# A gated DeltaNet layer: the state's update from plain transposed keys and a scaled y

## The chip, the cores and the metric

The kernel runs on one core of one Trainium2 chip. The metric is the device time of one execution in microseconds (us). The engines meant below are TensorE (PE in the rows, PEld where it loads weights), VectorE (DVE), ScalarE (ACT), GpSimd (POOL) and the queue of SyncE (SP), which issues most DMAs. Each engine executes its own instructions in a fixed order and waits on semaphores for the others.

## The reference, cut to what matters

The layer has two branches on the same normalised input: a Fourier branch, and a bidirectional gated DeltaNet with 8 heads of 128 channels. The context (256 tokens) is scanned first; the latent tokens (1024) start from its final states. Cut to one head, one direction and one chunk, the scan is this:

```python
def step(s, xs):
    q_c, k_c, u_c, w_c, qk_c, gc_c = xs
    v_new = u_c - einsum('cd,de->ce', w_c, s)
    o_c = einsum('cd,de->ce', q_c * exp(gc_c)[:, None], s) + einsum('ij,je->ie', qk_c, v_new)
    g_last = gc_c[-1]
    k_dec = k_c * exp(g_last - gc_c)[:, None]
    s = s * exp(g_last) + einsum('cd,ce->de', k_dec, v_new)
    return s, o_c
```

The last product sums over the tokens c of the chunk. The factor exp(g_last - gc_c) belongs to a token, so it may stand on the key's row or on the row of v_new: the sum is the same.

## The kernel before, in words

The kernel takes chunks of 128 tokens: 8 latent chunks (NCH) and 2 context chunks (NXC), 10 units (NU) in all. The big projections are products in three float32r passes (L127, L130 and L133, 128x512 each), which accumulate in two double-bank buffers called main. The work of a head's DeltaNet is float32.

Each head goes through three stages in `deltanet` (L671), which yields wherever TensorE may take other work:

1. **zp.** For five pairs of chunks, K K^T and K Q^T (L688) are multiplied by decay factors E into the tile zp (L692). The factors come by DMA (L708), get a mask on GpSimd (L710) and an exponential on ScalarE (L714).
2. **inverse** (L724). VectorE inverts 32x32 blocks in a loop of 30 steps (L748, L751), and TensorE puts the blocks together.
3. **scan** (L818). Ten steps t. Each serves direction 0 (d=0) from the front and direction 1 from the end, with a state S[d] each. t=0 and 1 are the context's chunks.

One scan step before the change, by line: L840 multiplies the keys by S; L842 (VectorE) makes R of it; L850 multiplies the queries by S, from t=2 on, into one PSUM bank for both directions (qs2); L854 multiplies the inverted block by R; L856 (ScalarE) copies that product, y, from PSUM into zp (at t=0 with a factor -1); L861 (ScalarE, t=2 to 5) or L863 (VectorE, t=6 to 9) scales the product of L850 into the output acc; L869 multiplies the keys kdec by y; L873 (VectorE) makes the new S of it; from t=6 on, L881 adds both directions' inner part out of zp. At t=9 no state is updated.

kdec is the tile of transposed keys times ce, the factor of the token: L699, on GpSimd, one instruction for each direction (128x1280), issued after the five pairs of zp and before the inverse. The plain transposed keys, ktok (L617), come from PSUM by VectorE (L622), and `k_norms` (L644 to 654) makes ce out of the decays, the gates and the keys' norms. These run for head h+1 while head h is worked on. Both ktok and kdec have one buffer.

PSUM has four banks of a ring called s for all the small products; a product gets the bank that was used four allocations before, once its readers are done.

What sets the order: `weave` (L248) hands out the projections of the next head and of the merge gates as fill between the steps of the head's own chain, by a table of times (STEPS, times a head's RATES). That gives the order in the code; the compiler's planner then orders each engine's instructions with its own costs, so that ready work further down in the code may be put ahead. In the trace the masks (L710) for head 1's first four pairs run before 376 us, although the code issues them inside head 0's scan, which begins at 413 us. The weights of the fill are loaded by `weight` (L178): DMA on SP (L182), a cast on ScalarE (L188), a subtraction on GpSimd (L189).

Of the kernel before, what the change touches and what calls it, by code (L numbers as in the profile page):

```python
# [8 lines left out]
F32 = mybir.dt.float32  # L9
# [54 lines left out]
class Net:  # L64
# [18 lines left out]
    def rsqrt(self, pool, x, shape, tag):  # L83
        """1 / sqrt(x) of a small float32 tile: Newton steps from an integer seed."""
        v = self.nc.vector
        y = pool.tile(shape, F32, tag=tag + "y", name=tag + "y")
        t = pool.tile(shape, F32, tag=tag + "t", name=tag + "t")
        v.tensor_scalar(out=t.bitcast(I32), in0=x.bitcast(I32), scalar1=1, scalar2=None,
                        op0=ALU.arith_shift_right)
        v.tensor_scalar(out=y.bitcast(I32), in0=t.bitcast(I32), scalar1=-1, scalar2=1597463007,  # L90
                        op0=ALU.mult, op1=ALU.add)
        for _ in range(3):
            v.tensor_tensor(out=t, in0=y, in1=y, op=ALU.mult)
            v.scalar_tensor_tensor(out=t, in0=t, scalar=-0.5, in1=x, op0=ALU.mult, op1=ALU.mult)
            v.scalar_tensor_tensor(out=y, in0=t, scalar=1.5, in1=y, op0=ALU.add, op1=ALU.mult)
        return y

    def split(self, x, hi, lo, eng=None):
        """x = hi + lo, both of float32r's width."""
        self.nc.scalar.copy(out=hi, in_=x)  # L100
        (eng or self.nc.gpsimd).tensor_tensor(out=lo, in0=x, in1=hi.bitcast(F32), op=ALU.subtract)  # L101

    def split2(self, x, hi, lo, n):
        """The same by halves, on two engines."""
        for c, e in ((slice(0, n // 2), self.nc.gpsimd), (slice(n // 2, n), self.nc.vector)):
            self.split(x[:, c], hi[:, c], lo[:, c], e)

    def operand(self, part):
        """One part of eight blocks of 128 rows by 1024, in the place of the last such."""
        return [self.hpool.tile([P, NT], F32R, tag=f"{part}{k}", name=f"{part}{k}") for k in range(KT)]  # L110

    def turns(self):
        """VectorE and GpSimd by turns."""
        self.turn = not self.turn
        return self.nc.vector if self.turn else self.nc.gpsimd

    def mm3(self, ps, lh, ll, rh, rl, first, last):
        """ps += (lh + ll)^T (rh + rl) in three float32r passes."""
        mm = self.nc.tensor.matmul
        mm(ps, lhsT=lh, rhs=rh, start=first, stop=False)  # L120
        mm(ps, lhsT=lh, rhs=rl, start=False, stop=False)
        mm(ps, lhsT=ll, rhs=rh, start=False, stop=last)

    def mm3y(self, ps, lh, ll, rh, rl, first, last):
        """The same, giving TensorE away in between."""
        mm = self.nc.tensor.matmul
        mm(ps, lhsT=lh, rhs=rh, start=first, stop=False)  # L127
        if FINE == 3:
            yield 0.217
        mm(ps, lhsT=lh, rhs=rl, start=False, stop=False)  # L130
        if FINE == 3:
            yield 0.217
        mm(ps, lhsT=ll, rhs=rh, start=False, stop=last)  # L133
        yield 0.65 if FINE == 1 else 0.216

# [1 line left out]
    def constants(self):  # L137
# [21 lines left out]
        # adds up four blocks of 32 rows  # L159
# [32 lines left out]
    def latent(self, src, rhs, k, done):  # L192
        """A block of weights times the latent tokens' operand: quanta of PE work, then done(PSUM)."""
# [24 lines left out]
    def plain(self, f):  # L218
        """Work that needs no weights, as a job."""
# [5 lines left out]
    def after(self, f):  # L225
        """The same for work in several parts."""
        return None, 0, lambda w: f()

    def stream(self, jobs, first=None):
        """Run jobs in order, the weights of the next one under way; first: the first one's, if they are."""  # L230
# [17 lines left out]
    def weave(self, lead, fill, rate, times):  # L248
        """fill takes TensorE between the lead's steps: after each, rate times its entry of times."""
# [12 lines left out]
    def pe_add(self, x, rows, ec, eng=None):  # L262
        """x += the tokens' position code: the grid's rows in one half of the channels, its columns in the other."""
# [3 lines left out]
    def head(self, first):  # L267
# [6 lines left out]
        with ExitStack() as es:  # L274
# [8 lines left out]
            # rows' codes in three parts of bfloat16's width, and which of them a token takes  # L283
# [31 lines left out]
            def parted(i):  # L315
                """A group's weights in two parts, in the place of operands to come or of tokens gone."""
# [8 lines left out]
            # silu of c and c_ctx  # L325
# [5 lines left out]
            # in two parts, all four columns against either part of the weights  # L331
# [49 lines left out]
            # scale and shift as columns, two contraction blocks at a time  # L381
# [42 lines left out]
            def narrow(ps, h, l, kt):  # L424
                """Rows 0-31 take two of the three products, 32-63 the third."""
# [45 lines left out]
    def tables(self, bd, sp):  # L471
# [5 lines left out]
        # turned, and the two parts added up  # L477
# [18 lines left out]
        # log1p(e) = 2 atanh(e / (2 + e))  # L496
# [15 lines left out]
        # running sums within a chunk, in each direction's order, and the whole chunk's  # L512
# [13 lines left out]
        # sums as rows  # L526
# [12 lines left out]
    def conv(self, pool, ps, blk, dst, n, view=None, bufs=4, parts=1, away=False):  # L539
        """dst = 2 silu(conv(ps)) along the free dim."""  # L540
# [43 lines left out]
    def tok(self, src, units):  # L584
        """Transposes of up to four chunks into one PSUM bank."""
# [10 lines left out]
    def qkv_jobs(self, h, G):  # L596
        """The head's projections and all of its preparation that needs no decay matrix."""
# [18 lines left out]
        def k_tok():  # L616
            G.ktok = dn.tile([P, NU, P], F32, tag="ktok", name="ktok")  # L617
# [11 lines left out]
        def q_tok():  # L629
# [9 lines left out]
            # the guard of the output's norm, in the units of the unnormalised q  # L639
# [4 lines left out]
        def k_norms():  # L644
# [7 lines left out]
            for d in range(2):  # L652
                v.tensor_tensor(out=G.c[:, d], in0=self.b[:, 8 * d + h], in1=r2, op=ALU.mult)
                v.tensor_tensor(out=G.ce[:, d], in0=self.edl[:, 8 * d + h], in1=G.c[:, d], op=ALU.mult)

# [15 lines left out]
    def deltanet(self, h, G, side):  # L671
        """Yields wherever TensorE may take other work meanwhile."""
# [3 lines left out]
        # decay factors, zero outside the triangle; [Z | P] = [K K^T | K Q^T] c E  # L676
# [20 lines left out]
        G.kdec = dn.tile([P, 2, NU, P], F32, tag="kdec", name="kdec")  # L697
        for d in range(2):
            gp.tensor_tensor(out=G.kdec[:, d], in0=G.ktok, in1=G.ce[:, d].unsqueeze(2).to_broadcast([P, NU, P]), op=ALU.mult)  # L699
# [3 lines left out]
    def decays(self, h, p):  # L703
        """A pair of chunks' decay factors, zero outside the triangle, in either direction."""
# [11 lines left out]
    def collect(self, G, lo, hi):  # L716
        """Diagonal 32-blocks of some chunks side by side, direction 1 transposed: all upper triangles."""
# [6 lines left out]
    def inverse(self, G, side):  # L724
        """Z -> V = -(I + strict Z)^-1 in place, both directions of all chunks."""
# [7 lines left out]
        # one block a partition: X[block, column, row]  # L733
# [4 lines left out]
        # a column's entries need only columns as they were: even and odd columns by turns  # L738
# [22 lines left out]
        # the halves' inverses, transposed  # L761
# [6 lines left out]
        # 32 -> 64  # L768
# [19 lines left out]
        # 64 -> 128  # L788
# [29 lines left out]
    def scan(self, h, G):  # L818
# [9 lines left out]
        for t in range(NU):  # L828
            if h + 1 < HEADS and t in EARLIER:
                self.decays(h + 1, EARLIER.index(t))  # L830
            # the context's two chunks, then the latent tokens'; direction 1 from the ends
# [20 lines left out]
            for d, u in enumerate(us):  # L852
                ps = self.s()[:, :P]
                mm(ps, lhsT=zp[:, d, u], rhs=R[d], start=True, stop=True)  # L854
                y[d] = zp[:, d, u]
                act.mul(out=y[d], in_=ps, mul=-1.0) if new else act.copy(out=y[d], in_=ps)  # L856
# [9 lines left out]
            if not last:  # L866
                for d, u in enumerate(us):
                    ps = self.s()[:, :P]
                    mm(ps, lhsT=G.kdec[:, d, u], rhs=y[d], start=True, stop=True)  # L869
# [23 lines left out]
    def finish(self, h, G):  # L893
        """RMS norm over the head's channels, q's norm with it; the gate. Yields between parts."""
# [34 lines left out]
    def fourier_jobs(self, sp, ctx):  # L929
# [19 lines left out]
        def fold(g, ps):  # L949
# [9 lines left out]
            # the cosine and sine sums of even k, then their even and odd ones; those of odd k  # L959
# [109 lines left out]
    def gate_rows(self, sp):  # L1069
        """adaLN's gate, halved, on every partition."""  # L1070
# [19 lines left out]
        # silu doubled: acc is twice the product  # L1090
# [7 lines left out]
    def heads_out(self):  # L1098
        """All heads' outputs as the operand of the next product, and its first blocks: jobs."""
# [18 lines left out]
    def tail(self):  # L1118
# [3 lines left out]
        with ExitStack() as es:  # L1122
# [21 lines left out]
            def gated(kt):  # L1144
                """Rows of the output weights, times adaLN's gate."""
# [21 lines left out]
            def source(i):  # L1167
                """Token tile i: what its product is added to, and where that goes, by column pieces."""
# [215 lines left out]
```

## Time and profile before

| what | value |
|---|---|
| three runs | 1408.75, 1407.92, 1408.34 us, median 1408.34 us |
| the profiled execution: its span, which is all that the page gives of its time | 1409.0 us |
| PE busy | 1296.9 us, 92% |
| DVE busy | 967.8 us, 69% |
| ACT busy | 555.9 us, 39% |
| POOL busy | 451.1 us, 32% |
| mean granted TensorE clock | 0.959 |

An engine's share is its busy time over the span and says nothing of what the other engines waited for. The views used below are the page, groups of instructions by line (with least, middle and greatest duration), sums of waits, the busy time in stretches, the timeline and the chain of work that ended last, which is followed back from the last instruction.

### The profile page before, as it was taken

How to read it: one execution, taken by the hardware profiler on the slowest of the kernel's cores; microseconds unless marked ns; L12 is line 12 of the kernel's file. 1: busy time of each engine (PE TensorE's matmuls, PEld its weight loads, DVE VectorE, ACT ScalarE, POOL GpSimd, SP SyncE). 2: the span in 40 equal slices, each digit the busy share in tenths (PEclk: the TensorE clock that was granted, in tenths of full speed). 3: DMA queues.
4: the chain of work that ended last, by engine and by line, in shares of the span. 5: the costliest groups of instructions: out<-in, count | busy, mean ns of one | idle time of the engine just before them, and what ended most of it. 6: DMA issues, size and time to landing. Idle time of an engine off the chain costs nothing.

```text
span 1409.0 us, 22686 instructions
## 1 busy us (share of the span) xinstructions
PE 1296.9 (92%) x8274; PEld 1050.7 (75%) x8274; DVE 967.8 (69%) x2664; ACT 555.9 (39%) x1499; POOL 451.1 (32%) x358
## 2 busy tenths in 40 slices
PE   7899999999789989889899998988998999999997
PEld 1487787887678768768777876876876877888786
DVE  6776554308876965984894795697697494744997
ACT  2643333335444444443544444345354343521200
POOL 3532332135523222430440332223243122234610
PEclk9999999999899999989998999999998999999999
DMA  8434332342211211311311211121120032375431
GB/s 316 152 97 119 115 111 91 125 169 78 65 39 44 69 46 48 88 61 38 83 58 56 53 62 66 50 79 54 35 79 31 31 113 75 120 264 162 160 124 60
DMA packets 51892, 129.91 MB, mean 92 GB/s; under 512 B 6242, under 2 KB 18915, under 8 KB 51780
## 3 DMA queue, kind: packets, MB, share of 16 engines
q1 hardware_dynamic: 44496, 114.02, 26.1%
q10 hardware_dynamic: 7284, 14.45, 3.0%
q8 instruction: 65, 1.06, 0.3%
q14 instruction: 47, 0.39, 0.1%
HBM read 105.29 MB, written 23.15 MB: 91 GB/s over the span
## 4 chain that ended last, share of the span: by engine, by line
PE 50%; DVE 33%; DMA 6%; ACT 5%; POOL 3%; issue 3%; ACTq 0%; SPq 0%; DVEq 0%; POOLq 0%
PE main L127 8%; PE main L133 8%; PE main L130 8%; DVE X L751 7%; DVE B L748 6%; DMA E<-gr 3%; PE s L854 3%; PE s L869 3%; PE s L840 2%; PE s L881 2%; PE s L850 2%; DVE cv L553 2%; POOL E L710 2%; DVE cv L552 2%; PE main L120 2%
## 5 line engine op out<-in xcount | busy, mean ns | idle before, releaser
L127 PE MATMUL main<-h,whi 128*128 128x512 f32 x1008 | 424.8, 421 | 6.2 <-DVE cv L553 6.2
L133 PE MATMUL main<-h,wlo 128*128 128x512 f32 x1008 | 410.8, 408 | 0.1
L130 PE MATMUL main<-l,whi 128*128 128x512 f32 x1008 | 410.2, 407 | 0.0
L127 PEld LDWEIGHTS main<-h,whi 128*128 128x128 f32 x1008 | 196.2, 195 | 42.9 <-ACT th L554 5.8
L189 POOL TENSOR_TENSOR wlo<-wraw,whi 128x1024 fp32r<-128x1024 f32 x48 | 127.7, 2660 | 307.1 <-ACT whi L188 295.0
L133 PEld LDWEIGHTS main<-h,wlo 128*128 128x128 f32 x1008 | 195.5, 194 | 40.5 <-POOL wlo L101 0.5
L130 PEld LDWEIGHTS main<-l,whi 128*128 128x128 f32 x1008 | 196.0, 194 | 32.8
L751 DVE TENSOR_TENSOR X<-X,B 128x110 f32<-128x110 f32 (+27 forms) x472 | 120.6, 292 | 0.0
L748 DVE TENSOR_TENSOR B<-X 128x110 f32<-128x110 f32 (+27 forms) x472 | 111.8, 274 | 0.0
L101 POOL TENSOR_TENSOR wlo<-wraw,whi 128x512 fp32r<-128x512 f32 (+1 forms) x40 | 49.8, 1245 | 180.9 <-ACT whi L100 172.2
L710 POOL TENSOR_TENSOR E<-E,mask 128x256 f32<-128x256 f32 x80 | 67.2, 866 | 89.7 <-DMA E<-gr 62.0
L188 ACT CAST whi<-wraw 128x512 fp32r<-128x512 f32 x96 | 59.4, 623 | 79.7 <-PE main L130 71.4
L100 ACT CAST whi<-wraw 128x512 fp32r<-128x512 f32 (+1 forms) x80 | 44.7, 575 | 109.1 <-PE main L130 73.5
L554 ACT ACTIVATE th<-cv 128x512 f32<-128x512 f32 (+1 forms) x64 | 36.9, 576 | 124.6 <-DVE cv L553 124.4
L714 ACT ACTIVATE E<-E,nG 128x128 f32<-128x128 f32 x160 | 52.7, 392 | 68.2 <-POOL E L710 67.7
L692 DVE SCALAR_TENSOR_TENSOR zp<-s,c,E 128x256 f32<-128x256 f32 (+1 forms) x160 | 64.5, 452 | 21.6 <-ACT E L714 14.6
L101 DVE TENSOR_TENSOR wlo<-wraw,whi 128x512 fp32r<-128x512 f32 (+1 forms) x40 | 36.9, 923 | 61.4 <-ACT whi L100 48.2
L699 POOL TENSOR_TENSOR kdec<-ktok,ce 128x1280 f32<-128x1280 f32 x16 | 37.0, 2326 | 130.6 <-PE s L869 128.3
L873 DVE SCALAR_TENSOR_TENSOR S<-S,egl,s 128x128 f32<-128x128 f32 x128 | 40.0, 344 | 54.9 <-PE s L869 53.2
L856 ACT COPY zp<-s 128x128 f32<-128x128 f32 x144 | 36.3, 273 | 80.3 <-PE s L854 80.3
L552 DVE SCALAR_TENSOR_TENSOR cv<-main,cst,cv 128x511 f32<-128x511 f32 (+1 forms) x48 | 35.3, 735 | 39.6 <-ACT cv L549 39.6
L842 DVE SCALAR_TENSOR_TENSOR R<-s,eG,vt 128x128 f32<-128x128 f32 x144 | 45.3, 347 | 22.5 <-PE s L840 19.1
(343 smaller groups left out, 2560.3 us busy)
## 6 DMA issues: line engine op xcount, KB each, us to landing
wraw<-in_win SPq DMA_DIRECT2D x72, 512.0 KB, 3.5
E<-gr SPq DMA_DIRECT2D x40, 256.0 KB, 4.7
wmod<-in_wm SPq DMA_DIRECT2D x32, 256.0 KB, 5.4
x<-in_x SPq DMA_DIRECT2D x8, 512.0 KB, 5.4
wgate<-in_wg SPq DMA_DIRECT2D x8, 512.0 KB, 3.9
yf<-yf ACTq DMA_DIRECT2D x8, 512.0 KB, 2.8
rfy<-yf SPq DMA_DIRECT2D x8, 512.0 KB, 4.5
af<-rfy SPq DMA_DIRECT2D x8, 512.0 KB, 2.6
```

Source lines behind the costliest of these rows:

```text
L101: (eng or self.nc.gpsimd).tensor_tensor(out=lo, in0=x, in1=hi.bitcast(F32), op=ALU.subtract)
L127: mm(ps, lhsT=lh, rhs=rh, start=first, stop=False)
L130: mm(ps, lhsT=lh, rhs=rl, start=False, stop=False)
L133: mm(ps, lhsT=ll, rhs=rh, start=False, stop=last)
L188: self.nc.scalar.copy(out=hi[:, i:i + n], in_=raw[:, i:i + n])
L189: self.nc.gpsimd.tensor_tensor(out=lo[:, :k], in0=raw[:, :k], in1=hi[:, :k].bitcast(F32), op=ALU.subtract)
L552: v.scalar_tensor_tensor(out=x[:, a:hi], in0=ps[:, a - 1:hi - 1], scalar=w(0), in1=x[:, a:hi], op0=ALU.mult, op1=ALU.add)
L692: v.scalar_tensor_tensor(out=o, in0=ps.rearrange("p (a i) -> p a i", a=W), scalar=G.c[:, d, u:u + 1], in1=e[:, d, i].unsqueeze(1).to_broad ...
L710: nc.gpsimd.tensor_tensor(out=e[:, d], in0=e[:, d], in1=self.mask[:, d].unsqueeze(1).to_broadcast([P, 2, P]), op=ALU.add)
L714: nc.scalar.activation(out=e[:, d, i], in_=e[:, d, i], func=AF.Exp, bias=self.nG[:, 8 * d + h, u:u + 1])
L748: v.tensor_tensor(out=B, in0=X[:, c0::2, l:l + 1].to_broadcast([P, w, l]), in1=X[:, l:l + 1, :l].to_broadcast([P, w, l]), op=ALU.mult)
L751: v.tensor_tensor(out=X[:, c0::2, :l], in0=X[:, c0::2, :l], in1=B, op=ALU.subtract)
```

## The change

The diff also strips comments and docstrings throughout; that part is left out here. ktok gets a second buffer, since it is now read until the end of the scan. ce gets a factor -1 in the two columns that t=0 uses. kdec goes. In the scan, y becomes a tile of its own with four buffers, written by ScalarE from PSUM with the factor ce of each token (each partition), for all steps but the last; the unscaled copy into zp remains for the latent chunks, as a second reading of the same bank. L869's product takes ktok and the scaled y.

```diff
         def k_tok():
-            G.ktok = dn.tile([P, NU, P], F32, tag="ktok", name="ktok")
+            G.ktok = dn.tile([P, NU, P], F32, tag="ktok", name="ktok", bufs=2)
...
                 v.tensor_tensor(out=G.ce[:, d], in0=self.edl[:, 8 * d + h], in1=G.c[:, d], op=ALU.mult)
 
+            for d, u in enumerate((NCH, NU - 1)):
+                v.tensor_scalar(out=G.ce[:, d, u:u + 1], in0=G.ce[:, d, u:u + 1], scalar1=-1.0, scalar2=None, op0=ALU.mult)
+
...
             yield
-        G.kdec = dn.tile([P, 2, NU, P], F32, tag="kdec", name="kdec")
-        for d in range(2):
-            gp.tensor_tensor(out=G.kdec[:, d], in0=G.ktok, in1=G.ce[:, d].unsqueeze(2).to_broadcast([P, NU, P]), op=ALU.mult)
         yield from self.inverse(G, side)
...
                 mm(ps, lhsT=zp[:, d, u], rhs=R[d], start=True, stop=True)
-                y[d] = zp[:, d, u]
-                act.mul(out=y[d], in_=ps, mul=-1.0) if new else act.copy(out=y[d], in_=ps)
+                if not last:
+                    y[d] = dn.tile([P, P], F32, tag="y", name="y", bufs=4)
+                    act.mul(out=y[d], in_=ps, mul=G.ce[:, d, u:u + 1])
+                if t >= NXC:
+                    act.copy(out=zp[:, d, u], in_=ps)
...
                     ps = self.s()[:, :P]
-                    mm(ps, lhsT=G.kdec[:, d, u], rhs=y[d], start=True, stop=True)
+                    mm(ps, lhsT=G.ktok[:, u], rhs=y[d], start=True, stop=True)
```

## Rows read from the trace of the kernel before

**Rows 1.** The page: the chain that ended last, by engine.
```profile
PE 50%; DVE 33%; DMA 6%; ACT 5%; POOL 3%; issue 3%; ACTq 0%; SPq 0%; DVEq 0%; POOLq 0%
```

**Rows 2.** Head 1's inverse and scan: us, PE, PEld, DVE, ACT, POOL busy; clock, DMA.
```profile
460.00:500.00 40.00, 35.84 (x155) 28.85 (x153) 39.97 (x144) 17.20 (x51) 11.54 (x10) 0.91 0.24 72
...
520.00:560.00 40.00, 40.00 (x311) 35.12 (x310) 18.65 (x54) 15.93 (x50) 5.68 (x3) 1.00 0.10 34
```

**Rows 3.** By line: kdec; y's copies; ScalarE's scaled reading of PSUM (ns, min/median/max).
```profile
L699 POOL TENSOR_TENSOR kdec<-ktok,ce x16: 2319/2326/2331, 334.3 to 1125.2; 128x1280 f32<-128x1280 f32 x16
...
L856 ACT COPY zp<-s x144: 256/267/360, 417.0 to 1227.2; 128x128 f32<-128x128 f32 x144
...
L861 ACT ACTIVATE acc<-s,eG x64: 367/380/452, 419.5 to 1209.5; 128x128 f32<-128x128 f32 x64
```

**Rows 4.** Sums of waits: who <- whom, us in total, times, longest.
```profile
PEld s L869 <- ACT zp L856: 7.7, 36, 0.6
```

**Rows 5.** Timeline of head 0, t=3: start, duration, instruction, [idle before <- releaser].
```profile
422.47 0.37 ACT L861 ACTIVATE acc<-s,eG 128x128 f32<-128x128 f32 x1 [1.99 <-PE s L850]
...
422.73 0.26 ACT L856 COPY zp<-s 128x128 f32<-128x128 f32 x1
422.88 0.38 ACT L861 ACTIVATE acc<-s,eG 128x128 f32<-128x128 f32 x1
423.04 0.30 PEld L869 LDWEIGHTS s<-zp,kdec 128*128 128x128 f32 x2 [0.20 <-ACT zp L856]
...
423.14 0.28 ACT L856 COPY zp<-s 128x128 f32<-128x128 f32 x1
...
423.29 0.48 PE L127 MATMUL main<-h,whi 128*128 128x512 f32 x1
...
423.61 0.38 PE L869 MATMUL s<-zp,kdec 128*128 128x128 f32 x2
```

**Rows 6.** Timeline of head 1, t=7.
```profile
550.85 0.49 ACT L856 COPY zp<-s 128x128 f32<-128x128 f32 x2 [4.27 <-PE s L854]
...
551.57 0.60 PE L869 MATMUL s<-zp,kdec 128*128 128x128 f32 x4
```

**Rows 7.** Timeline of GpSimd between heads 1 and 2.
```profile
556.70 2.33 POOL L699 TENSOR_TENSOR kdec<-ktok,ce 128x1280 f32<-128x1280 f32 x1 [20.54 <-PE s L869]
558.99 2.36 POOL L189 TENSOR_TENSOR wlo<-wraw,whi 128x1024 fp32r<-128x1024 f32 x1
...
568.55 2.80 POOL L710 TENSOR_TENSOR E<-E,mask 128x256 f32<-128x256 f32 x4 [4.92 <-DMA E<-gr]
```

**Rows 8.** The chain that ended last, at the same place: start, duration, link.
```profile
562.83 0.89 DVE zp L692 x2
563.74 4.68 DMA E<-gr
```

**Rows 9.** Timeline of GpSimd, VectorE and ScalarE ahead of head 0.
```profile
334.31 4.62 POOL L699 TENSOR_TENSOR kdec<-ktok,ce 128x1280 f32<-128x1280 f32 x2 [2.36 <-DVE ce L654]
338.88 2.83 POOL L189 TENSOR_TENSOR wlo<-wraw,whi 128x1024 fp32r<-128x1024 f32 x1
...
337.94 1.54 DVE L562 SCALAR_TENSOR_TENSOR vT<-th,cv 128x512 f32<-128x512 f32 x1
...
341.22 1.04 DVE L562 SCALAR_TENSOR_TENSOR vT<-th,cv 128x512 f32<-128x512 f32 x1
...
335.48 0.62 ACT L188 CAST whi<-wraw 128x512 fp32r<-128x512 f32 x1
```

**Rows 10.** Timeline of VectorE and GpSimd while head 3's keys are normalised.
```profile
619.40 2.32 DVE L88 TENSOR_SCALAR dnrt<-se 128x10 int32<-128x10 int32 x1
...
624.21 0.25 DVE L654 TENSOR_TENSOR ce<-edl,c 128x10 f32<-128x10 f32 x2
...
627.80 0.68 DVE L562 SCALAR_TENSOR_TENSOR vT<-th,cv 128x512 f32<-128x512 f32 x1
...
619.30 2.39 POOL L189 TENSOR_TENSOR wlo<-wraw,whi 128x1024 fp32r<-128x1024 f32 x1
```

## The prediction

> **What bounds the kernel now.** First the chain by engine [rows 1]: half of the span is TensorE, a third VectorE, 5% ScalarE and 3% GpSimd. The two engines whose work the change alters most are thus hardly on the chain, so I read the stages. The stretches [rows 2] show two limits that take turns in each head. In the inverse VectorE is busy 39.97 of 40.00 us and TensorE 35.84. In the scan TensorE is busy 40.00 of 40.00, VectorE 18.65, ScalarE 15.93, GpSimd 5.68, at a granted clock of 1.00. The scan is therefore bound by TensorE's queue as long as fill stands ready for each wait of the chain L840, L842, L854, L856, L869, L873. Whether it always does is told by the sum of waits [rows 4]: L869's weight load waited for y 36 times, 7.7 us in all, 0.21 each, in 72 steps that update a state. Two steps show both kinds. In head 0, t=3 [rows 5], the first y ends at 422.99 and L869 starts at 423.04, 0.20 late; the second y ends at 423.42, and one product of the fill lies between L869's two halves. In head 1, t=7 [rows 6], both copies are done by 551.34 and L869 starts at 551.57: 0.23 us to spare.
>
> **GpSimd: kdec goes.** It is 16 x 2.326 = 37.2 us of GpSimd [rows 3], but what is it worth on the chain? Between heads 1 and 2 [rows 7] kdec waited until the old scan's last reading of it, and the subtraction of the next weights, wlo, stands between its two halves: that wlo comes at most 2.33 us earlier without it, and SP's next load of raw weights, which waits for wlo's reading, with it. GpSimd's next work is the mask at 568.55, which waits for a DMA; that DMA leaves when VectorE releases its buffer at 563.72 [rows 8]. kdec is not what is late there, nor is GpSimd. I take zero for heads 1 to 7; a gain is bounded by one kdec half in the four heads with this pattern, 9.3 us.
>
> Head 0 is different [rows 9]. Its kdec runs from 334.31 to 338.93, and VectorE's v convolution L562 at 337.94 took 1.54 us, against 0.68 elsewhere [rows 10]; the next one, beside wlo (338.88 to 341.71), took 1.04. Without kdec, wlo starts when its cast ends, at 336.10, and ends about 338.5. The first L562 is then done near 338.5 + 0.55 = 339.05 instead of 339.48 (0.43 gained), the second runs free (0.36 gained). The v convolution is on the chain there, ahead of the first product of zp: -0.8 us, between 0 and -1.2 (both excesses, 0.86 + 0.36, gone).
>
> The Trainium skill ("SBUF — State Buffer", section "SBUF: two separate sides") says that GpSimd and VectorE share a pair of ports under an exclusive lock: a VectorE operation with two SBUF inputs, or in a two-port mode, waits for the whole of a GpSimd one. The trace agrees: L88, an instruction of 128x10 elements, took 2.32 us beside a wlo of 2.39 [rows 10]. The rule speaks for a gain wherever such an operation runs beside kdec. In heads 1 to 7 the timeline has only L873, L842, L863, L882, L568 and L692 there, which read PSUM and keep their usual durations; so the rule adds nothing to the 0.8 us of head 0.
>
> **VectorE: two columns of ce change sign.** Two instructions on one column for each head, 16 in all. The trace has none on one column; the nearest are the two L654 on ten columns, 0.25 us as a pair [rows 10]. I take 0.2 us for the new pair. For heads 1 to 7 they stand in VectorE's queue ahead of the v convolution and the joining of the 64-blocks, on the chain in most of them: 6 x 0.2 = +1.2 us. Bounds: 0 (all in gaps) and 8 x 0.25 = 2.0; one that meets a GpSimd instruction could cost up to 2.3 like L88, and I leave that to the range.
>
> **ScalarE: y scaled, then copied.** Steps t=2 to 8 get two instructions more, 14 for each head, 112 in all: 112 x 0.267 = 30 us more busy time on an engine that is busy 15.93 of 40 us in the scan. The busy time costs nothing by itself; the place in the queue does. Reading PSUM with a factor per partition takes 380 ns against the copy's 267 [rows 3], so the first y comes 0.11 us later. The second y now has the first unscaled copy ahead of it. From the starts in [rows 5], the next instruction begins 0.26 us after a scaled one (422.47 to 422.73) and 0.15 after a copy (422.73 to 422.88). Put into that step: the acc product at 422.47, y at 422.73, the copy at 422.99, the second acc product at 423.14, the second y at 423.40, done at 423.78. Its half of L869 started at 423.61 before and can now start at about 423.83: +0.22. If the planner puts the second acc product behind both copies, the bank of qs2 comes free only when that is done, and the fourth-next allocation is L869's second bank: y at 423.14, copy 423.40, acc 423.55 to 423.93, so 423.98: +0.37. If it puts both y ahead of both copies, only some +0.1 remains.
>
> Where there is 0.23 us to spare, as in [rows 6], this is covered; nothing of L881 moves, since it stands behind L869. Where y is already awaited, in 36 steps, between 36 x 0 and 36 x 0.37 = 13.3 us could show. Another fill product of 0.23 us put into the hole takes most of it, at the price of having less fill later; what stays visible today is 0.21, less than one such product. I take a third of 0.22 + 0.02 = 0.08 for each: +2.9 us. If the cover were gone in all 56 steps from t=2 to 8, it would be 56 x 0.22 = 12.3.
>
> The rest costs nothing: L869 does the same product on other weights, loaded the same way; y has four buffers, two steps' worth; the second ktok is written while the first is read, so the copies L622 wait for nothing new.
>
> **Sum.** Against the span: 1409.0 - 0.8 + 1.2 + 2.9 = 1412.3 us. The median of the runs shown is 0.7 us below that span, so 1411.6 us for the runs.
>
> **The rivals.**
> - *Covered.* The planner moves fill into every hole, as it already does between L869's halves in [rows 5], or puts both y first; what is left is 1.2 - 0.8: 1408.7 us. For it: TensorE has no gap in head 1's scan [rows 2]. Against: y is awaited in half of the steps [rows 4].
> - *Faster, by the ports.* Taking kdec away moves wlo, up to 2.33 us, and where the order of GpSimd's later work shifts against the keys' norms, the 2.1 us that L88 lost (2.32 against the 0.25 of two such small instructions) in heads like that of [rows 10] go: four heads, 8.4 us, so 1411.6 - 8.4 = 1403.2 us; from two heads on it is faster than before. Against: the wlo in question, at 619.30, stands in the inverse behind other GpSimd work, 58 us after kdec. (Were all of kdec's 37.2 us taken off VectorE's share of the chain, it would be 1409.0 - 37.2 - 0.7 = 1371.1 us; only head 0's kdec shows a held-up neighbour, so I give that 0.01, within this rival's chance.)
> - *Slower, by ScalarE's queue.* The copies stand ahead of the second acc product, qs2 is held, and each step from t=2 to 5 is 0.37 us longer with the fill used up: 32 x 0.37 = 11.8, with 9 awaited steps from t=6 on at 0.22 another 2.0: 1409.0 - 0.8 + 1.2 + 13.8 - 0.7 = 1422.5 us. It decides as soon as ten such steps show it (3.7 us). For it: the code has the copies ahead of the acc products. Against: the acc product's bank is ready before y's is [rows 5], and TensorE's fill stands at hand.
> - *The change not doing what it says*: none that I see, since kdec's instructions are simply absent.
>
> **Numbers.** The measurement tells some 0.2% (2.8 us) from no change. Forecast (slightly slower, 1409.5 to 1416): 0.42, of which 0.1 lies within 0.2%. Covered: 0.24, within. Ports: 0.18, faster. ScalarE's queue: 0.16, slower. So faster 0.18, same 0.34, slower 0.48. The range goes from 1404 (just under half of the port rival's gain against today's time) to 1420 (most of ScalarE's queue): about 0.1 is left out at either end.
>
> **What would show it.** In the trace after: no L699; the wait of L869's load for y longer than 7.7 us in all, up to 10 or 11; y at 0.38 us and the second y some 0.25 us later against L854 than before; in head 0, L562 near its 0.68; L88 near 2.3 still. The prediction is wrong if the total of those waits is unchanged or if the stretch from one scan to the next shrinks; if the scan of heads 1 to 4, where fill covers y today, grows by over 1 us each, ScalarE's queue or the planner's order is the cause.

## The result and the profile after

The changed kernel takes 1416.79 us (median of four runs, 1414.57 to 1420.08; the kernel before beside it 1408.13). The ratio is 1.0075, with a 95% interval of 1.0052 to 1.0098: slower by 0.75%. The profiled execution spans 1418.3 us, 9.3 more than before, at a granted clock of 0.961 (0.959 before).

The page of the changed kernel, busy time by engine, then the chain that ended last by engine (against [rows 1]):

```profile
PE 1297.2 (91%) x8274; PEld 1047.4 (74%) x8274; DVE 967.8 (68%) x2680; ACT 586.5 (41%) x1611; POOL 408.8 (29%) x342
...
PE 36%; DVE 23%; DMA 3%; ACT 3%; issue 1%; POOL 1%; DVEq 0%; ACTq 0%; POOLq 0%; SPq 0%
```

GpSimd has lost 42.3 us of busy time (451.1 before) and ScalarE has gained 30.6; TensorE and VectorE do what they did. The chain's shares add up to 67% here, since it was not followed back to the start, so they are not set against [rows 1].

By line of the changed kernel (count, ns min/median/max), against [rows 3]. L857 writes the scaled y, L859 the copy into zp, L864 is what was L861, L657 the change of sign:

```profile
L857 ACT ACTIVATE y<-s,ce x144: 349/368/415, 414.7 to 1231.4; 128x128 f32<-128x128 f32 x144
L857 ACTq EVENT_SEMAPHORE  x104: 17/17/17, 420.4 to 1220.2; - x104
...
L859 ACT COPY zp<-s x128: 255/266/308, 420.7 to 1236.0; 128x128 f32<-128x128 f32 x128
...
L864 ACT ACTIVATE acc<-s,eG x64: 359/398/432, 420.2 to 1216.3; 128x128 f32<-128x128 f32 x64
...
L657 DVE TENSOR_SCALAR ce<-ce x16: 141/154/155, 334.8 to 1078.7; 128x1 f32<-128x1 f32 x16
```

kdec's line is gone. The second row was in nobody's sum: 104 of the 144 scaled readings come with an event of their own in ScalarE's queue. In the program those 104 wait for two things, TensorE's product and an earlier instruction of ScalarE itself, because y's tile is reused in turn; in the kernel before no y has such an event.

The sum of waits of the load of L872 (before: L869) for y, against [rows 4]:

```profile
PEld s L872 <- ACT y L857: 11.1, 44, 1.0
```

That is 3.4 us more. It is only a part. **Where the 9.3 us lie** is told by the stages. Take a head's scan from the first L854 of t=0 to that of t=9:

| scan of head | 0 | 1 | 2 | 3 | 4 | 5 | 6 | 7 | sum |
|---|---|---|---|---|---|---|---|---|---|
| before, us | 27.38 | 34.07 | 34.08 | 34.08 | 34.36 | 30.06 | 26.59 | 35.57 | 256.2 |
| after, us | 29.75 | 34.71 | 34.75 | 34.69 | 34.70 | 31.61 | 28.41 | 36.94 | 265.6 |

The scans have grown by 9.4 us, the whole difference. All that lies ahead of the scans in their heads went from 613.2 to 612.7, the start from 343.0 to 342.8, the end behind the last scan from 182.4 to 183.0; the 14.2 us between a scan's last step and the next head's first product are unchanged. Each figure comes from one execution. The scans repeat well (256.2 before, 256.3 in e1_no_kdec below, which leaves the order in the scan alone), but the start, which hardly differs between the kernels of this document, ranges from 339.9 to 344.2 us.

Counted in the trace, 16 more products of the fill stand in the scans (414 against 398; 7 more in head 0, 4 in head 5, 5 in head 6). Their number does not set the growth: e2_scaled_only, below, has 11 more than before (409), and its scans grow by 0.8 us.

The 9.4 us are not all of one kind. Steps t=6 to 8 of heads 0, 5 and 6 carry 3.6 of them; of these, 0.81 lie in head 0, t=6, where 7 products of the fill stand instead of 3 and the second y begins 1.86 us after the step's first L854 instead of 0.69. And of head 7's 1.4 us, 1.08 lie in t=8, where a cast ahead of y in ScalarE's queue waited for a DMA, so that the first y begins 2.33 us after the first L854 instead of 0.67. No term of the prediction has that wait, and no run here shows whether the change caused it:

```profile
1230.47 0.62 ACT L100 CAST h<-wraw 128x512 fp32r<-128x512 f32 x1 [2.77 <-DMA wraw<-og]
1230.99 0.36 ACT L857 ACTIVATE y<-s,ce 128x128 f32<-128x128 f32 x1
```

Heads 1 to 4 grew little. Busy time by engine (PE, PEld, DVE, ACT, POOL; then clock, DMA) in the same 35 us of head 1's scan, first after, then before (the wider stretch is in [rows 2]):

```profile
528.00:563.00 35.00, 35.00 (x244) 31.23 (x243) 18.26 (x53) 17.50 (x57) 4.02 (x2) 1.00 0.11 39
```

```profile
524.00:559.00 35.00, 35.00 (x248) 31.41 (x247) 18.36 (x54) 13.75 (x44) 4.68 (x3) 1.00 0.12 39
```

TensorE is "busy 35.00 of 35.00" in both, yet it got through 244 rows where it had got through 248. Full busy time did not mean that a late y was covered.

Head 0, t=3 of the changed kernel, to be laid beside [rows 5]:

```profile
423.29 0.37 ACT L864 ACTIVATE acc<-s,eG 128x128 f32<-128x128 f32 x1 [1.59 <-PE s L850]
...
423.49 0.47 PE L127 MATMUL main<-h,whi 128*128 128x512 f32 x1
423.57 0.37 ACT L857 ACTIVATE y<-s,ce 128x128 f32<-128x128 f32 x1
...
423.80 0.40 PE L130 MATMUL main<-l,whi 128*128 128x512 f32 x1
423.83 0.26 ACT L859 COPY zp<-s 128x128 f32<-128x128 f32 x1
423.98 0.38 ACT L857 ACTIVATE y<-s,ce 128x128 f32<-128x128 f32 x1
423.99 0.72 PEld L872 LDWEIGHTS s<-y,ktok 128*128 128x128 f32 x4 [0.22 <-ACT y L857]
...
424.38 0.40 ACT L864 ACTIVATE acc<-s,eG 128x128 f32<-128x128 f32 x1
```

The second acc product has moved behind both y. The first L872 comes 0.70 us after the first acc product's start (0.57 before), with two fill products ahead of it, and still waits. The second y ends 1.07 after that start (424.36); before it was 0.95.

The places where kdec and the sign were priced, ahead of head 0 (against [rows 9, 10]), VectorE:

```profile
334.76 0.23 DVE L657 TENSOR_SCALAR ce<-ce 128x1 f32<-128x1 f32 x2
...
338.43 1.19 DVE L562 SCALAR_TENSOR_TENSOR vT<-th,cv 128x512 f32<-128x512 f32 x1
...
341.35 0.64 DVE L562 SCALAR_TENSOR_TENSOR vT<-th,cv 128x512 f32<-128x512 f32 x1
```

and GpSimd there:

```profile
336.66 2.40 POOL L189 TENSOR_TENSOR wlo<-wraw,whi 128x1024 fp32r<-128x1024 f32 x1 [4.22 <-ACT whi L188]
```

and GpSimd between heads 1 and 2 (against [rows 7]):

```profile
561.34 2.36 POOL L189 TENSOR_TENSOR wlo<-wraw,whi 128x1024 fp32r<-128x1024 f32 x1 [20.80 <-ACT whi L188]
```

The two L562 lost 0.35 and 0.40 us. Between heads 1 and 2 GpSimd now stands idle for 20.80 us until its cast comes. That wlo is earlier than before: it starts 1.63 us ahead of the first L854 of t=9, before 0.28 behind it. But GpSimd's next work, the mask, comes 9.83 us behind that L854, before 9.84: it still waits for its DMA.

### The profile page after: what moved, and what is told of

Read it like the earlier page. It is cut to its first block, busy times and chain, and to the rows that moved or that the text cites. A ratio compares the mean times of both kernels' runs of the same rounds, so it can differ in the third digit from the quotient of the medians.

```text
span 1418.3 us, 22951 instructions
## 1 busy us (share of the span) xinstructions
PE 1297.2 (91%) x8274; PEld 1047.4 (74%) x8274; DVE 967.8 (68%) x2680; ACT 586.5 (41%) x1611; POOL 408.8 (29%) x342
## 4 chain that ended last, share of the span: by engine, by line
PE 36%; DVE 23%; DMA 3%; ACT 3%; issue 1%; POOL 1%; DVEq 0%; ACTq 0%; POOLq 0%; SPq 0%
PE main L127 6%; PE main L133 6%; PE main L130 6%; DVE B L748 5%; DVE X L751 4%; PE s L872 2%; PE s L854 2%; PE s L840 2%; DMA E<-gr 2%; PE s L884 2%; PE s L850 2%; DVE cv L552 1%; PE main L122 1%; PE main L120 1%; PE main L121 1%
## 5 line engine op out<-in xcount | busy, mean ns | idle before, releaser
L748 DVE TENSOR_TENSOR B<-X 128x110 f32<-128x110 f32 (+27 forms) x472 | 121.1, 291 | 0.0
L751 DVE TENSOR_TENSOR X<-X,B 128x110 f32<-128x110 f32 (+27 forms) x472 | 117.0, 283 | 0.0
L876 DVE SCALAR_TENSOR_TENSOR S<-S,egl,s 128x128 f32<-128x128 f32 x128 | 41.6, 345 | 61.6 <-PE s L872 59.7
L857 ACT ACTIVATE y<-s,ce 128x128 f32<-128x128 f32 x144 | 52.0, 374 | 59.8 <-PE s L854 59.7
L872 PEld LDWEIGHTS s<-y,ktok 128*128 128x128 f32 x288 | 44.2, 188 | 16.9 <-ACT y L857 11.1
```

Source lines behind the costliest of these rows:

```text
L748: v.tensor_tensor(out=B, in0=X[:, c0::2, l:l + 1].to_broadcast([P, w, l]), in1=X[:, l:l + 1, :l].to_broadcast([P, w, l]), op=ALU.mult)
L751: v.tensor_tensor(out=X[:, c0::2, :l], in0=X[:, c0::2, :l], in1=B, op=ALU.subtract)
L872: mm(ps, lhsT=G.ktok[:, u], rhs=y[d], start=True, stop=True)
```

## The experiments

All are timed in five rounds against the kernel before, which was run again beside them; so it is the ratios that can be compared between rows. "Scans" is the sum above (256.2 before, 265.6 after).

| run | us | ratio, 95% interval | scans |
|---|---|---|---|
| e1_no_kdec | 1406.27 | 0.9992, 0.9980 to 1.0004 | 256.3 |
| e2_scaled_only | 1406.7 | 0.9992, 0.9977 to 1.0007 | 257.0 |
| e3_extra_copy | 1409.2 | 1.0012, 1.0001 to 1.0023 | 259.0 |
| e4_copies_last | 1417.13 | 1.0066, 1.0048 to 1.0085 | 262.6 |
| e5_scaled_copied | 1414.19 | 1.0042, 1.0028 to 1.0055 | 262.2 |
| e6_own_tile | 1408.63 | 1.0003, 0.9989 to 1.0018 | 257.8 |
| e7_copy_vectore | 1415.95 | 1.0046, 1.0029 to 1.0063 | 263.9 |
| e8_acc_vectore | 1405.98 | 0.9981, 0.9966 to 0.9997 | 255.7 |
| e9_second_y_vectore | 1409.66 | 1.0021, 1.0008 to 1.0033 | 263.3 |
| e10_y_acc_vectore | 1414.47 | 1.0045, 1.0029 to 1.0061 | 264.9 |
| e11_in_place | 1414.05 | 1.0046, 1.0030 to 1.0062 | 260.7 |
| e12_in_place_acc | 1408.09 | 1.0002, 0.9987 to 1.0018 | 259.1 |

**kdec alone away.** From the kernel before; L869 reads ktok.

```diff
-        G.kdec = dn.tile([P, 2, NU, P], F32, tag="kdec", name="kdec")
-        for d in range(2):
-            gp.tensor_tensor(out=G.kdec[:, d], in0=G.ktok, in1=G.ce[:, d]...)
...
-                    mm(ps, lhsT=G.kdec[:, d, u], rhs=y[d], start=True, stop=True)
+                    mm(ps, lhsT=G.ktok[:, u], rhs=y[d], start=True, stop=True)
```

> The kernel before, with kdec taken away and nothing put in its place: ktok (two buffers, its evacuation on VectorE scaled by the constant 0.001) is read by L869 as it is, so the decays and gates are missing from the state's update; GpSimd's 37 us are gone, ScalarE's part is as before. Theory (the place of the extra copies in ScalarE's queue makes the scan longer, removing kdec gives only head 0's 0.8 us): 1407.4 us, scans as before to 0.2 us each, L562 ahead of head 0 near 1.2 and 0.65 us. Rival (removing GpSimd's work shifts the planner's order, and that is where the 8.7 us come from): 1412 us or more, spread over stages other than the scan.

0.9992: 37 us of GpSimd's time are worth about 1 us, 2.8 at most by the interval, which includes no change.

**The scaled reading alone.** The kernel before without kdec, L869 on plain ktok, and y scaled by ce in its old place, no second copy.

```diff
-                act.mul(out=y[d], in_=ps, mul=-1.0) if new else act.copy(out=y[d], in_=ps)
+                act.copy(out=y[d], in_=ps) if last else act.mul(out=y[d], in_=ps, mul=G.ce[:, d, u:u + 1])
```

> The kernel before without kdec, with y scaled by ce on leaving PSUM and written to zp in place, so there is no second copy; the part of the output that reads zp gets the scaled y, which is not what it should read. This leaves the change without its 112 extra copies. Theory (the copies' place in the queue): each y only 0.11 us later, scans +0.2 to +1 us each where y is awaited, 1409 to 1411 us. Rival (the slower scaled reading, 380 against 267 ns, is what costs): 1414 us or more, scans nearly as long as in the changed kernel (29.8 us for head 0, 28.4 for head 6).

No change of the time that the interval shows, scans +0.8: less than the theory's price, and far from the rival's.

**The copy alone.** The kernel before, with one more reading of the bank behind each y.

```diff
+                if NXC <= t and not last:
+                    spare = dn.tile([P, P], F32, tag="spare", name="spare")
+                    act.copy(out=spare, in_=ps)
```

> The kernel before, kdec and unscaled y kept, with one more ScalarE copy of the same bank (t=2 to 8, 112 in all) into a tile that nobody reads, issued behind each y as the changed kernel does. Theory (the copies' place in the queue): the second y 0.15 to 0.26 us later, 1412 to 1415 us, scans of heads 0 and 6 longer by 1 to 1.6 us each. Rival (the scaled reading): at most +1 us, 1408 to 1409.

Less than the theory expected and near its rival's figure: +0.12%, scans +2.8. Neither part explains +0.75%, and both together would give scans +3.6, not +9.4.

**Both copies behind both y**, in the changed kernel.

```diff
-                if t >= NXC:
-                    act.copy(out=zp[:, d, u], in_=ps)
+            if t >= NXC:
+                for d, u in enumerate(us):
+                    act.copy(out=zp[:, d, u], in_=yp[d])
```

> The changed kernel with the two unscaled copies issued behind both y, in the order of the code. Theory (the copies' place in the queue): second y 0.15 us earlier than in the changed kernel, 1410 to 1413 us. Rival (the scaled reading): as the changed kernel, 1416 us. If the planner still puts a copy ahead of the second y, since that is not ready when ScalarE becomes free, it stays near 1416 as well, and the trace shows that order.

A miss: no gain against the changed kernel that the intervals show, though scans fell by 3.0 us. In head 6 the steps from t=6 on fell from 3.48 to 3.31 us; those of t=2 to 5 stayed at 3.09.

**Scaled reading and copy together**, y in its old place: the edit of the second experiment with that of the third.

> The kernel before without kdec, y scaled by ce in its old place in zp (the output's product then reads the scaled y), and behind each y of steps 2 to 8 a ScalarE copy of the same bank into a tile that nobody reads: ScalarE's work is that of the changed kernel, y's place is the old one. Theory A (scaling and copy together push y over another fill product, neither alone): 1414 to 1417 us, scans 7 to 9 us longer than before, the second L869 of steps 6 to 8 at 1.3 us after the step's first zp.R product. Theory B (y in a tile of its own is what costs: its instructions come with one more semaphore event and start 0.06 us later): 1407 to 1410 us, scans 3 to 4 us longer.

Scans +6.0, more than +0.8 and +2.8 together: the first theory's direction, though short of its 7 to 9. The changed kernel, which has y's own tile as well, is at +9.4; but 1.2 of these last 3.4 us lie in head 7, most of them in the step that waits behind a DMA (t=8: 5.54 us here, 6.67 there).

**y in its own tile, no copy**: the changed kernel with `if last:` for `if t >= NXC:` ahead of the copy.

> The changed kernel without its copies into zp before the last step (the output's product of steps 2 to 8 reads the inverse there in y's place): y scaled, in a tile of its own. Theory A (scaling and copy together): 1406 to 1409 us, scans within 2 us of before. Theory B (y's own tile): 1411 to 1415 us, scans 4 to 6 us longer, y's start 0.48 us after the step's first zp.R product against 0.42. Theory C (the copy alone, by ScalarE's queue): 1407 to 1409 us.

By itself again almost nothing: 1.0003, scans +1.6. Yet its y begins 0.06 us later, as the rival said. So three small things, each free or nearly so alone, stand in a kernel that loses 0.75%. **How they add up** is seen in one step of head 6, t=7. The kernel before:

```profile
1118.11 0.68 PE L854 MATMUL s<-R,zp 128*128 128x128 f32 x4
...
1118.57 0.52 ACT L856 COPY zp<-s 128x128 f32<-128x128 f32 x2 [2.63 <-PE s L854]
1118.88 0.56 PEld L869 LDWEIGHTS s<-zp,kdec 128*128 128x128 f32 x4 [0.18 <-ACT zp L856]
```

The same step of e5_scaled_copied:

```profile
1120.94 0.68 PE L851 MATMUL s<-R,zp 128*128 128x128 f32 x4
...
1121.40 0.37 ACT L853 ACTIVATE zp<-s,ce 128x128 f32<-128x128 f32 x1 [1.44 <-PE s L851]
...
1121.67 0.26 ACT L856 COPY spare<-s 128x128 f32<-128x128 f32 x1
...
1121.81 0.38 ACT L853 ACTIVATE zp<-s,ce 128x128 f32<-128x128 f32 x1
1121.82 0.72 PEld L869 LDWEIGHTS s<-zp,ktok 128*128 128x128 f32 x4 [0.17 <-ACT zp L853]
```

And of the changed kernel:

```profile
1124.81 0.69 PE L854 MATMUL s<-R,zp 128*128 128x128 f32 x4
...
1125.34 0.37 ACT L857 ACTIVATE y<-s,ce 128x128 f32<-128x128 f32 x1 [1.50 <-PE s L854]
...
1125.60 0.26 ACT L859 COPY zp<-s 128x128 f32<-128x128 f32 x1
1125.75 0.38 ACT L857 ACTIVATE y<-s,ce 128x128 f32<-128x128 f32 x1
1125.76 0.72 PEld L872 LDWEIGHTS s<-y,ktok 128*128 128x128 f32 x4 [0.23 <-ACT y L857]
```

Read the starts against that of the zp.R product (L854, L851 in e5). Before, the second y begins about 0.72 us behind it (two copies in 0.52), just when ScalarE comes free of the first. A scaled first y keeps it there (the next instruction begins 0.27 later). A copy between them alone moves it to 0.78. Both make 0.46 + 0.27 + 0.14 = 0.87, and y's own tile, whose first y begins at 0.53 instead of 0.46, makes 0.93 or 0.94. What a copy, a scale and a wait add stands in one line ahead of the second y. And the step then pays all of it:

| head 6, t=7 | second y, us after the zp.R product's start | step, us | step less the second y's end |
|---|---|---|---|
| before | 0.72 to 0.99 | 3.15 | 2.16 |
| e3: copy | 0.78 to 1.07 | 3.23 | 2.16 |
| e2: scaled | 0.73 to 1.09 | 3.25 | 2.16 |
| e6: scaled, own tile | 0.79 to 1.15 | 3.32 | 2.17 |
| e4: all, copies last | 0.79 to 1.15 | 3.31 | 2.16 |
| e5: scaled and copy | 0.87 to 1.25 | 3.42 | 2.17 |
| after: all three | 0.93 to 1.31 | 3.48 | 2.17 |

From the second y's end to the next step everything is one chain (the second half of L872, the eight passes of L884 in TensorE's fixed order, L840, R, L854), 2.16 to 2.17 us in these seven kernels. It does not matter that the step holds one product of the fill before and in e3, and two in the others. In heads 1 to 4, whose steps of 4.45 us hold more fill, the same t=7 went from 4.45 to 4.52 only.

**The copies on VectorE**, in the changed kernel.

```diff
-                    act.copy(out=zp[:, d, u], in_=ps)
+                    (act.copy if last else v.tensor_copy)(out=zp[:, d, u], in_=ps)
```

> The changed kernel with its copies into zp on VectorE, but for the last step's. Theory A with ScalarE's queue as the place (the second y stands behind the first one's copy): the second y starts some 0.15 us earlier and the time falls to 1409 to 1412 us. Rival (the banks are held until the copy has read them, whoever copies): 1414 to 1418 us. A second rival: the copies stand ahead of the state's update in VectorE's queue and delay it: 1418 to 1424 us.

Head 6 falls as the first theory said (3.48 to 3.32 at t=7, 3.09 to 3.01 at t=3), but in heads 1 to 4 the scan grows from 34.7 to 35.1: in head 1, step 2 goes from 3.29 to 4.09 with three more products of the fill in it, and step 3 from 3.60 to 3.00 with two fewer. That is later, as the second rival said, but whether VectorE's queue or the planner's order does it was not shown. Together 1.0046, with an interval that overlaps the changed kernel's.

**The first acc products on VectorE**, in the kernel before.

```diff
-                    act.mul(out=acc[:, u], in_=qs[d], mul=col(self.eG, d, u))
+                    v.tensor_scalar(out=acc[:, u], in0=qs[d], scalar1=col(self.eG, d, u), scalar2=None, op0=ALU.mult)
```

> The kernel before, with the first product for acc (steps 2 to 5, between or behind the two y on ScalarE) on VectorE. If a step pays for each 0.1 us that y is late, as the changed kernel seems to: second L869 of steps 2 to 5 some 0.2 us earlier, 32 such steps, 1403 to 1406 us. If other work takes the time in between: 1407 to 1409 us. If VectorE's queue is then late for the state's update: 1409 to 1412 us.

0.9981: the one version here whose interval lies below the kernel before, by 0.03 to 0.34%. Among twelve versions one interval that misses 1 so narrowly can be chance. In head 6, t=3, with the acc product no longer between the two y, the second y ends at 0.96 us instead of 1.15, and the step takes 2.72 us against 2.93. ScalarE in that step of the kernel before:

```profile
1106.64 0.26 ACT L856 COPY zp<-s 128x128 f32<-128x128 f32 x1
1106.79 0.38 ACT L861 ACTIVATE acc<-s,eG 128x128 f32<-128x128 f32 x1
1107.05 0.28 ACT L856 COPY zp<-s 128x128 f32<-128x128 f32 x1
```

and of this run:

```profile
1106.03 0.52 ACT L856 COPY zp<-s 128x128 f32<-128x128 f32 x2 [2.20 <-PE s L854]
```

The scans' sum falls by only 0.5 us, since head 0 lost at t=7 (4.09 against 3.35) most of what it had gained; where the rest of the 2.2 us between the medians came from was not settled.

**The second y on VectorE**, in the changed kernel, then the acc products too.

```diff
-                    act.mul(out=y[d], in_=ps, mul=G.ce[:, d, u:u + 1])
+                    (v.tensor_scalar(out=y[d], in0=ps, scalar1=G.ce[:, d, u:u + 1], scalar2=None, op0=ALU.mult) if d else
+                     act.mul(out=y[d], in_=ps, mul=G.ce[:, d, u:u + 1]))
```

> The changed kernel with direction 1's y scaled by VectorE and direction 0's still by ScalarE; the copies stay on ScalarE. Theory (the second y stands in line on ScalarE behind y 0 and its copy, and with no slack each instruction ahead of it makes the step longer): the second y ends near 1.1 us after the step's first zp.R product against 1.31, the last L872 pass moves from 1.58 to about 1.4, the steps of head 6 fall from 3.09 and 3.48 to about 2.95 and 3.3, scans 2 to 4 us over before, 1410 to 1412 us. Rival 1 (banks held by the copies set the step): scans as in the changed kernel, 1415 to 1418 us. Rival 2 (VectorE's queue is late instead, above all in heads 1 to 4, as where it took the copies): 1412 to 1416 us with heads 1 to 4 longer than 34.7 us.

> The same, with the first products for acc (steps 2 to 5) on VectorE too. Theory (ScalarE's line): steps 2 to 5 of heads 0 and 6 fall to 2.75 to 2.9 us, the rest as in the run beside it, 1407 to 1411 us. Rival (VectorE now makes the second y late behind acc's two products, 0.26 us each): steps 2 to 5 no shorter than 2.95 and 1411 to 1414 us.

The second y came early as forecast (0.73 to 1.07 at t=7), but the step is 3.51, not 3.3. The timeline of the first of the two runs at that step says why:

```profile
1115.68 0.68 PE L854 MATMUL s<-R,zp 128*128 128x128 f32 x4
...
1116.40 0.35 DVE L857 TENSOR_SCALAR y<-s,ce 128x128 f32<-128x128 f32 x1
...
1116.66 0.45 PE L873 MATMUL s<-y,ktok 128*128 128x128 f32 x2
...
1116.87 0.47 PE L133 MATMUL main<-h,wlo 128*128 128x512 f32 x1
...
1117.18 0.38 PE L873 MATMUL s<-y,ktok 128*128 128x128 f32 x2
```

The planner put a fill product between the two halves of L873, and the second half starts 0.43 us after its y is done. Where it put none (e9, t=3) the step is 2.94, as in the kernel before; in e10 it put one there as well, and t=3 takes 3.12. So a fill product between the halves does lengthen the step (2.43 us from the second y's end, where the others have 2.16), and the order that the planner chose beforehand decides whether there is one. In e9 the scans hold 30 fill products more than before and grow by 7.1 us, yet the time grows by only 0.21%: ahead of the scans its heads need 607.0 us against 613.2, in the changed kernel 612.7. Whether that is fill given back is not shown: it is one execution of each, and the start alone differs by as much as 4.3 us between executions.

**The places swapped**: scaled y in zp, the unscaled copies in tiles of their own and behind both y; then the acc products on VectorE as well.

```diff
-                    y[d] = dn.tile([P, P], F32, tag="y", name="y", bufs=4)
+                    y[d] = zp[:, d, u]
...
+                    yo[d, u] = dn.tile([P, P], F32, tag="yo" + i, name="yo" + i, bufs=1 if i else 2)
+                    act.copy(out=yo[d, u], in_=yp[d])
...
-                        mm(ps, lhsT=zp[:, e, NU + u], rhs=zp[:, e, u], start=e == 0, stop=e == 1)
+                        mm(ps, lhsT=zp[:, e, NU + u], rhs=yo[e, u], start=e == 0, stop=e == 1)
```

> The changed kernel with the places swapped and the order mended: the scaled y goes into y's old place in zp, the unscaled copies go into tiles of their own (the output's product reads those), and both copies stand behind both y. If the changed kernel's loss is made of three parts, the scaled read (0.10 us a step), the copy ahead of the second y (0.14 to 0.17) and the wait on ScalarE's own semaphore that a reused tile brings (0.06), only the first is left: steps of head 6 from t=6 at 3.25 us, those of t=2 to 5 at 2.90 to 3.0, scans 1 to 3 us over before, 1407 to 1410 us. Rival (the copies hold the banks, wherever they write): steps of t=2 to 5 stay at 3.09, scans 4 to 6 us over before, 1411 to 1415 us.

> The same with the first products for acc (steps 2 to 5) on VectorE. If ScalarE's line ahead of the second y is all: steps of t=2 to 5 in head 6 at 2.75 to 2.85 us, scans within 1 us of before, 1405 to 1408 us, a form of the change that is no slower than the kernel before. If VectorE's two products make something else late: as the run beside it or slower.

From t=6 on both take the 3.25 us that was forecast for the first. At t=2 to 5 the first stays at 3.06, so its rival holds there and the time is 1.0046. Head 6, t=3 of e11_in_place:

```profile
1106.85 0.65 PE L855 MATMUL s<-R,zp 128*128 128x128 f32 x4
...
1107.32 0.62 ACT L858 ACTIVATE zp<-s,ce 128x128 f32<-128x128 f32 x2
...
1107.73 0.71 PEld L876 LDWEIGHTS s<-zp,ktok 128*128 128x128 f32 x4 [0.20 <-ACT zp L858]
...
1107.82 0.44 ACT L863 COPY yo<-s 128x128 f32<-128x128 f32 x2
1108.12 0.41 ACT L868 ACTIVATE acc<-s,eG 128x128 f32<-128x128 f32 x1
```

and of e12_in_place_acc:

```profile
1102.15 0.65 PE L855 MATMUL s<-R,zp 128*128 128x128 f32 x4
...
1102.36 0.61 DVE L868 TENSOR_SCALAR acc<-s,eG 128x128 f32<-128x128 f32 x2
...
1102.58 0.63 ACT L858 ACTIVATE zp<-s,ce 128x128 f32<-128x128 f32 x2 [1.93 <-PE s L855]
...
1103.00 0.56 PEld L876 LDWEIGHTS s<-zp,ktok 128*128 128x128 f32 x4 [0.17 <-ACT zp L858]
1103.11 0.42 ACT L863 COPY yo<-s 128x128 f32<-128x128 f32 x2
```

In e11 the four loads of L876 take 0.71 us, in e12 0.56. The second half starts 1.29 us after the zp.R product in e11, 0.20 after its y's end and 0.05 after the first copy's end (1.24); in e4_copies_last it was 1.32, again 0.05 after the first copy's end. In e12 it starts at 1.17, before the first copy ends (1.21): VectorE is done with qs2 by 0.81, so another bank was free. This fits a bank that the first copy still holds while qs2 waits behind the copies for ScalarE. No row names the bank, so that is inferred.

With all of it mended the change costs nothing that the interval shows (1.0002), and gains nothing either. The expectation for e12 was met only nearly: t=2 to 5 take 2.87 to 2.89 us in head 6, the time is 1408.09, and the scans are 2.9 us over before, 1.2 of them in head 7. e8, which keeps kdec and mends only the acc products, has the lowest ratio here, but its interval overlaps that of e12.

## Why the prediction came out as it did

The forecast was 1411.6 us, 3.3 more than before; measured were 1416.79, 8.7 more. The direction and the range (1404 to 1420) were right, but the time lies just above the band that the prediction gave its own mechanism (1409.5 to 1416).

- **kdec away: -0.8 in head 0, zero elsewhere. Held in the trace.** The two L562 lost 0.75 us. The Trainium skill ("SBUF — State Buffer", section "SBUF: two separate sides") lets a VectorE operation on two SBUF inputs wait out a GpSimd one; the trace agrees: the first L562 still takes 1.19 us and ends 0.56 after wlo's end (339.06). That was in the sum, but the list of signs had it "near its 0.68". e1 puts the whole at 0.9992, with 2.8 us of gain at most, so the ports' rival (8.4 us) is out. Whether the 0.75 us shows in the time can't be told.
- **Sign change: 0.2 for a pair.** 0.23 measured. The trace of before did have instructions on one column, against what the prediction says: eight L1216, 0.15 us each at the median, as each new L657. Whether the 1.2 us showed in the time can't be told, as the stages ahead of the scans did not grow.
- **y scaled, then copied: +2.9. This term was mis-sized**: the scans grew by 9.4, some 8 of it without the DMA wait in head 7. The engine and the place were right. In the step that was worked through (head 0, t=3) the planner took another order, with the second acc product behind both y: against the first L854 the second y starts 0.02 us later, not 0.26, and ends 0.12 later, and the step grew by 0.16. At t=7 of head 6, which has no acc product on ScalarE, it starts 0.21 later and ends 0.32 later, and the step grew by 0.33. The piece that failed is "another fill product of 0.23 us put into the hole takes most of it", with a third of it visible. Fill was put in (16 products), but that uses TensorE's idle time and does not shorten the chain: from the second y's end to the next step it is 2.16 to 2.17 us with one product in the step or with two. Where few products stand in a step, the step is late by all that y is late. Nor did only the 36 awaited steps pay: 51 of the 72 steps grew by more than 0.05 us. (Of those 36, by the trace, 9 are at t=0 and 1, where no copy was added, and 8, not 9, from t=6 on.) Heads 0, 5 and 6 carry 5.7 of the 9.4 us. The wait on ScalarE itself was not counted at all.
- **The view that misled** is [rows 2]: TensorE busy 40.00 of 40.00 was read as cover. It is busy 35.00 of 35.00 in both kernels while it does less. The 0.23 us to spare in [rows 6] was right for steps with much fill: in heads 1 to 4 t=7 grew by only 0.07 us.
- **The rival "ScalarE's queue"** had the right engine and the nearer price (13.8 us against 9.4). Its mechanism, the bank of qs2 held by the later acc product, was not seen in the changed kernel: in head 0, t=3, the acc product did move behind both copies and ends at 424.78, but the second half of L872 had begun at 424.41, 0.05 us after the second y's end. There the second y came last. A bank held by ScalarE's later work is inferred only for e4 and e11, above.
- **"What would show it"** held in the main: the wait for y at 11.1, y at 0.37, L88 still at 2.32 at the longest, no scan of heads 1 to 4 over 1 us longer. It did not for the first L562 (1.19).

## What to carry to other kernels

In a recurrence of two directions served by one engine, the second one's link is the one to time: follow when it ends in each kernel. Where a step holds one or two products of the fill (t=6 to 8 of heads 5 and 6), it was that end plus a constant (2.16 us), and 2.43 where a product was put behind that end. Where a step held six (t=7 of heads 1 to 4), a second y that ended 0.36 us later cost 0.07. Taking 37 us off an engine that is hardly on the chain gave about 1 us, with an interval that includes no change, while a slower reading, a copy and a wait in one line ahead of that link, 0.32 us at t=7 of head 6, lengthened such steps by as much. Work that only shares the queue (the acc products, the unscaled copies) belongs behind the link or on another engine, with an eye on the PSUM bank that it then holds.

## What the runs showed of the hardware that was not expected

- On ScalarE the next instruction begins 0.26 to 0.27 us after a scaled reading of 128x128 that takes 0.37, and 0.14 to 0.15 after a copy that takes 0.26: the durations overlap, and it is the distances between starts that add up.
- A tile that is reused in turn by the same engine brings a second wait, for that engine itself, and with it an event of 17 ns; y then begins 0.06 us later at t=7 of head 6 (e6 against e2; 0.01 at its t=3), although the earlier instruction was long done.
- VectorE's scaled reading of the same 128x128 from PSUM takes 0.35 us and its next one begins 0.27 later: no faster than ScalarE, it only has another line.
